# Chunk recurrence of a head pair: full 128x128 products with zero blocks, copies shared with ScalarE, state scaling on GpSimd

## The chip, the cores and the metric

The kernel runs on one core of a Trainium2 chip. The metric is the device time in microseconds (us) of one launch, as the median of several runs. TensorE does the matrix products (the profile calls it PE, and its weight loads PEld), VectorE is DVE, ScalarE is ACT, GpSimd is POOL, and SyncE (SP) issues the transfers.

## What is computed

One layer of a hybrid decoder trunk on 512 tokens of width 2048, all in float32: RMSNorm, one wide input projection, three groups of heads that work on parts of it, a SiLU gate on each, one output projection, and the residual. The change concerns the first group, twelve RWKV-7 heads of width 64. Cut to what matters:

```python
def reference(x, norm_g, w_in, ...):
    h = _rms(x, norm_g[l])
    proj = h @ w_in[l]                       # 2048 -> 7296 columns
    ...
    ya = _rwkv7(r, k, v, wd, ad, ...) * silu(ga)     # 12 heads of 64
    yb = _pool(pu, pool_w, pool_scale) * silu(pg)
    yc = _stick_breaking(qc, kc, vc, ...) * silu(gc) # 12 heads of 64
    return x + concatenate([ya, yb, yc]) @ w_out[l]

# in _rwkv7, for every token t and head:
sa    = state @ (-kk_t)
state = state * w_t + outer(sa, kk_t * a_t) + outer(v_t, k_t)
y_t   = state @ r_t
```

## The kernel before

**The foreground.** The projections are products of float32r numbers: every weight tile and the hidden state are split into a high and a low part, and three products per tile make the sum (`three`, line 396). The input projection is worked on tile by tile, 128 columns wide; a tile is 48 products of 512 columns into one PSUM bank (`pj`). Weights come by halves of a tile through SP's queue (`raw`); ScalarE casts the high part (`wh`) and VectorE subtracts for the low part (`wl`).

**The branches.** Between any two foreground products the program may insert a step of a branch. Each branch is a Python generator that yields the time at which its next step may join TensorE's queue (`need`, line 346); `pump` (line 359) runs those that are due. The clock for this is `Pace` (line 90), a rough account of every engine's work, kept while the program is written down. The order of the instructions thus comes from its costs, and a scheduler may move them further by priority; on the chip each engine works through its queue in that order.

**The recurrence.** Heads are taken in six pairs (`rwkv`, line 488); on the 128 partitions the first head of a pair has the low 64 (`lo`), the second the high 64 (`hi`). The 512 tokens are cut into 8 chunks of 64. Ahead of the recurrence, the products within a chunk (`gm`, line 571, four chunks to a bank) give the tiles `lt`, `rx` and part of `amr`; a triangular inverse is worked out in `lt`. The chunks then follow each other (line 669). Per chunk and head:

- `w`: `amr` by the state and values in `uv` (line 674); VectorE copies it to `wsb` (676).
- `se`: the state scaled by the chunk's decay, on VectorE (680).
- `y`, first half: the state by the r part of `amr` (684).
- `u`: `lt` by `wsb` (687); VectorE copies it into `uv` (689).
- `s`: `bkt` by `uv` (694); VectorE adds it to `se` and writes the next state into `uv` (696).
- `y`, second half: `uv` by `rx` (698); ScalarE copies it out to `yc` (699).

So w, u, s and the next w form a chain through TensorE and VectorE. Each product is 64 columns wide with 64 weights columns, one for each head; the two heads use different halves of the array. The PSUM tag `c` has three banks, shared by w, y, u and s.

Of the kernel before, what the change touches and what calls it, by code (L numbers as in the profile page):

```python
# [26 lines left out]
# columns of the packed per-channel vectors  # L27
# [14 lines left out]
# columns of the packed constants  # L42
# [8 lines left out]
# column tiles of the input projection, in the order in which they are worked on  # L51
NFIRST = 3
BANKS = {"pj": 2, "g": 3, "c": 3}
# [36 lines left out]
class Pace:  # L90
    """A rough clock of the engines, kept while the program is written down: it tells when a step of a
    branch can join TensorE's queue without TensorE having to wait for it."""
# [59 lines left out]
    def matmul(self, out, lhsT, rhs):  # L152
        n = self.free(rhs)
        m = self.free(lhsT)
        if rhs.dtype == F32R:
            c = max(n / 2400.0, m * 0.00083)
        else:
            c = max(4 * max(n, 64) / 2400.0, 0.1) * (0.6 if m <= 64 or rhs.shape[0] <= 64 else 1.0)
        self.now += c + 0.004
        self.ready[self.key(out)] = self.now + 0.28  # L160
# [20 lines left out]
class Timed:  # L181
    """An engine whose instructions the clock takes note of."""
# [21 lines left out]
def hybrid_trunk_kernel(ctx: ExitStack, tc: tile.TileContext, x, xT, w_in, w_out, vecs, consts, up_w, pool_w, out, tap=None):  # L204
# [64 lines left out]
    nvec = cp.tile([P, 14], F32, name="nvec")  # -w0, -a0, qn * 1/8  # L269
# [14 lines left out]
    # TensorE's clock rises while the first loads are under way  # L284
# [4 lines left out]
    # the input goes to places that the branches need only later  # L289
# [3 lines left out]
    for pl, tag, parts in ((ap, "q2", 1), (ap, "k2", 1), (ap, "w3", 1), (rp, "bk", 2), (rp, "bkt", 2), (rp, "rx", 2),  # L293
                           (rp, "uv", 2), (rp, "amr", 3), (ap, "wt", 2)):
        xt = pl.tile([P, parts, T], F32, tag=tag, name=name("x"))
# [192 lines left out]
    def rwkv(p):  # L488
# [54 lines left out]
        amr = rp.tile([P, NC_, 3, C], F32, tag="amr", name=name("amr"))  # L543
        for h, s in ((0, lo), (1, hi)):
# [7 lines left out]
        dve.tensor_tensor(amr[:, :, 2, :], r3, e[:, :, 1:], ALU.mult)  # L552
# [7 lines left out]
        lt = rp.tile([P, NC_, C], F32, tag="lt", name=name("lt"))  # L560
        ms = strict.rearrange("p (o t) -> p o t", o=1)
        mi = incl.rearrange("p (o t) -> p o t", o=1)
        for half in range(2):
            cs = slice(4 * half, 4 * half + 4)
            for h, s, other in quad:
                yield need(*([amr, bk] if half == 0 and h == 0 else []), tag="g")
                g = gb("gm")
                for j in range(4):
                    cc = 4 * half + j
                    rhs = amr[s, cc, 0:3:2, :] if h == 0 else amr[s, cc, 1:3, :]  # L570
                    mm(g[:, j * P:(j + 1) * P], bk[s, cc, :, :], rhs)
                g4 = g.rearrange("p (c a t) -> p c a t", c=4, a=2)
                dve.tensor_tensor(lt[s, cs, :], g4[s, :, 0, :], ms[s].to_broadcast([HD, 4, C]), ALU.mult)
# [6 lines left out]
        for h in range(2):  # L580
            for b in range(2):
                r0 = h * HD + b * B
                dma(out=s1v[:, :, h, b, :], in_=lt[r0:r0 + B, :, b * B:(b + 1) * B])
# [7 lines left out]
        # inverse of the 32 x 32 diagonal blocks, one block to a partition  # L591
        # (four copies of each block, every copy working on every fourth row)
# [21 lines left out]
        for h in range(2):  # L614
            for b in range(2):
                r0 = h * HD + b * B
                dma(out=lt[r0:r0 + B, :, b * B:(b + 1) * B], in_=s2v[:, :, h, b, :])

        # meanwhile: bonus, value token-major
# [20 lines left out]
        # merge to the 64 x 64 inverse: X12 = X1 N12 X2  # L640
        xt = tmp("xt")
        dve.transpose(xt, lt.rearrange("p c t -> p (c t)"))
        xt3 = xt.rearrange("p (c t) -> p c t", t=C)
# [3 lines left out]
        for cc in range(NC_):  # L647
            for h in range(2):
                r0 = h * HD
                mm(q1[r0 + B:r0 + 2 * B, cc * B:(cc + 1) * B], lt[r0:r0 + B, cc, B:C], xt3[r0:r0 + B, cc, 0:B])  # L650
# [5 lines left out]
        for cc in range(NC_):  # L656
            for h in range(2):
                r0 = h * HD
                mm(q2[r0:r0 + B, cc * B:(cc + 1) * B], w1[r0 + B:r0 + C, cc * B:(cc + 1) * B], lt[r0 + B:r0 + C, cc, B:C])
        for h in range(2):  # L660
            r0 = h * HD
            dve.tensor_copy(out=lt[r0:r0 + B, :, B:C], in_=q2[r0:r0 + B, :NC_ * B].rearrange("p (c t) -> p c t", t=B))

        # the state, chunk by chunk
# [4 lines left out]
        for cc in range(NC_):  # L669
            last = cc + 1 == NC_  # L670
            yield need(amr, uv, tag="c", margin=TIGHT)
            wps = cb("w")
            for h, s, o in quad:
                mm(wps[s, 0:C], amr[:, cc, h, :], uv[:, cc, h, :])
            wsb = rp.tile([P, C], F32, tag="wsb", bufs=2, name=name("wsb"))
            dve.tensor_copy(out=wsb, in_=wps[:, 0:C])
            if not last:
                se = rp.tile([P, C], F32, tag="se", bufs=2, name=name("se"))
                for h, s, o in quad:
                    dve.tensor_scalar(se[s, :], uv[s, cc, h, :], ec[s, cc:cc + 1], None, ALU.mult)  # L680
# [351 lines left out]
```

## Time and profile before

| | before |
|---|---|
| median of 3 runs | 1101.93 us (1100.72 to 1106.57) |
| span of the profiled execution, its own time | 1100.3 us |
| TensorE busy | 1074.3 us |
| VectorE busy | 751.3 us |
| ScalarE busy | 427.0 us |
| GpSimd busy | 168.7 us |
| mean granted TensorE clock | 0.982 |

The profile is of one execution. The span runs from its first instruction to its last; the page gives no longer time for that execution, and it lies 1.6 us under the median of the runs. A product of fp32 operands leaves two records in the trace, one of float32r leaves one, and a transpose leaves one. A record lasts from its start to the end of its results, so records overlap; how long TensorE is taken by something is read from the distance between starts.

### The profile page before, as it was taken

Reading aid. Unit: us, or ns where it says so; the run is one execution under the profiler, and the core shown is the slowest. Engines: PE = TensorE matmul, PEld = TensorE weight load, DVE = VectorE, ACT = ScalarE, POOL = GpSimd, SP = SyncE. Lnnn points to the kernel's source line nnn. Section 1 sums busy time; section 2 is a strip of 40 time slices with the busy share of each in tenths; the row PEclk is TensorE's granted clock in tenths of the full one; section 3 lists DMA queues with packets and bytes.
Section 4 is the critical chain, followed back from the end, with each engine's and each line's share of the span. In section 5 each row is a group of like instructions: output and inputs, shape, how many; then the busy total and the mean of one; then the engine's idle time right before and its main releaser. Section 6 shows DMA issues by size and latency. Waiting matters only on the chain.

```text
span 1100.3 us, 14737 instructions
## 1 busy us (share of the span) xinstructions
PE 1074.3 (98%) x5552; PEld 804.6 (73%) x5552; DVE 751.3 (68%) x1589; ACT 427.0 (39%) x670; POOL 168.7 (15%) x223
## 2 busy tenths in 40 slices
PE   9898989999999999999999999999999999999998
PEld 7676765677766877668775787667876677888886
DVE  5676876788877797877977788777986457233232
ACT  7362434244452453434543345423454235111111
POOL 2641122111121011210111102111012111000000
PEclk9899998999999999899998999999999999999999
DMA  8122321133211322113311133112331124444232
GB/s 316 38 82 82 101 73 40 57 82 101 77 54 42 104 82 87 39 59 106 86 63 58 60 103 87 63 39 68 115 92 58 39 85 161 161 153 134 96 136 75
DMA packets 57031, 97.70 MB, mean 89 GB/s; under 512 B 29184, under 2 KB 30592, under 8 KB 56960
## 3 DMA queue, kind: packets, MB, share of 16 engines
q1 hardware_dynamic: 56960, 96.76, 27.8%
q8 instruction: 44, 0.72, 0.3%
q14 instruction: 27, 0.22, 0.1%
HBM read 90.98 MB, written 5.77 MB: 88 GB/s over the span
## 4 chain that ended last, share of the span: by engine, by line
PE 73%; DVE 10%; issue 4%; POOL 2%; ACT 1%; DMA 1%; SPq 0%; POOLq 0%; DVEq 0%
PE pj L338 43%; PE oacc L338 15%; PE o L338 2%; DVE w L198 2%; PE z L338 2%; PE gm L338 2%; DVE wl L198 2%; PE y L338 2%; PE w L338 1%; POOL e L198 1%; PE u L338 1%; PE wT L342 1%; DVE xblk L198 1%; DVE pr L198 1%; PE s L338 1%
## 5 line engine op out<-in xcount | busy, mean ns | idle before, releaser
L338 PE MATMUL pj<-hh,wl 128*128 128x512 f32 x864 | 351.7, 407 | 1.0 <-DVE wl L198 1.0
L338 PE MATMUL pj<-hh,wh 128*128 128x512 f32 x864 | 350.0, 405 | 2.7 <-ACT wh L198 2.7
L338 PE MATMUL pj<-hl,wh 128*128 128x512 f32 x864 | 352.3, 408 | 0.0
L198 DVE TENSOR_TENSOR wl<-raw,wh 128x1024 fp32r<-128x1024 f32 x140 | 174.0, 1243 | 151.6 <-ACT wh L198 145.1
L198 ACT CAST wh<-raw 128x1024 fp32r<-128x1024 f32 x140 | 146.9, 1049 | 332.6 <-PE pj L338 204.2
L338 PEld LDWEIGHTS pj<-hh,wh 128*128 128x128 f32 x864 | 164.7, 191 | 39.3 <-issue 3.6
L338 PEld LDWEIGHTS pj<-hh,wl 128*128 128x128 f32 x864 | 164.4, 190 | 38.1 <-DVE wl L198 2.1
L338 PEld LDWEIGHTS pj<-hl,wh 128*128 128x128 f32 x864 | 164.3, 190 | 36.2 <-issue 1.4
L198 POOL TENSOR_SCALAR e<-e 128x512 f32<-128x512 f32 x28 | 49.3, 1760 | 365.0 <-ACT e L198 364.7
L338 PE MATMUL oacc<-wl,yh 128*128 128x512 f32 x256 | 100.2, 391 | 0.8 <-DVE wl L198 0.8
L338 PE MATMUL oacc<-wh,yh 128*128 128x512 f32 x256 | 99.7, 389 | 0.0
L338 PE MATMUL oacc<-wh,yl 128*128 128x512 f32 x256 | 99.7, 389 | 0.0
L198 POOL TENSOR_TENSOR d<-u 128x512 f32<-128x512 f32 x25 | 34.1, 1363 | 214.0 <-DVE u L198 178.9
L338 PEld LDWEIGHTS oacc<-wl,yh 128*128 128x128 f32 x256 | 48.1, 188 | 11.4 <-DVE wl L198 1.2
L338 PEld LDWEIGHTS oacc<-wh,yl 128*128 128x128 f32 x256 | 48.1, 188 | 10.2 <-issue 0.2
L338 PEld LDWEIGHTS oacc<-wh,yh 128*128 128x128 f32 x256 | 48.1, 188 | 9.8
L198 ACT ACTIVATE e<-e 128x512 f32<-128x512 f32 x50 | 31.5, 629 | 43.8 <-POOL e L198 43.4
L198 DVE TENSOR_TENSOR xblk<-xblk,pr 128x60 f32<-128x60 f32 (+8 forms) x180 | 42.0, 233 | 4.3
L198 DVE TENSOR_TENSOR_SCAN w<-kon,n 128x512 f32<-128x512 f32 (+3 forms) x48 | 39.4, 848 | 7.9 <-POOL n L198 7.6
L198 DVE TENSOR_TENSOR u<-pj,rstd 128x512 f32<-128x512 f32 x50 | 34.3, 686 | 13.9 <-PE pj L338 13.8
L198 DVE TENSOR_TENSOR pr<-xblk,nblk 128x60 f32<-128x60 f32 (+8 forms) x180 | 40.3, 224 | 4.5
L198 ACT ACTIVATE n<-n 128x512 f32<-128x512 f32 (+1 forms) x72 | 39.0, 557 | 1.3
(195 smaller groups left out, 1300.6 us busy)
## 6 DMA issues: line engine op xcount, KB each, us to landing
raw<-in_w_in SPq DMA_DIRECT2D x108, 512.0 KB
raw<-in_w_out SPq DMA_DIRECT2D x32, 512.0 KB
xr<-in_x SPq DMA_DIRECT2D x16, 256.0 KB
out<-xr SPq DMA_DIRECT2D x16, 256.0 KB
fr<-in_w_in SPq DMA_DIRECT2D x12, 256.0 KB
nblk<-s SPq DMA_DIRECT2D x24, 128.0 KB
x<-in_xT SPq DMA_DIRECT2D x5, 512.0 KB
x<-in_xT SPq DMA_DIRECT2D x3, 256.0 KB
```

The costliest lines, as they stand in the source:

```text
L198: return call(*args, **kw)
L338: pe.matmul(o, lhsT, rhs, start=start, stop=stop)
L342: pe.transpose(o, src, ident)
```

## The change

The tiles are laid out so that one product serves both heads of a pair. `amr` becomes 128 x 8 x 4 x 64, with zeros where a head's block would meet the other head's rows; `lt` gets a second block per head, zero outside the head's own rows. Both are allocated once for all pairs; the blocks that stay zero are filled once, and GpSimd clears the two others for every pair. In each chunk w, u, s and the two halves of y are one product each: 128 rows, 128 weight columns, and 128 columns streamed (64 for u). w, u and s of a chunk share one bank (`wus`, tag `c`, now two banks); y of four chunks shares the one bank of a new tag `y`, and is copied out once in four chunks. VectorE copies the first head's half of w and u, ScalarE the second's. `se` is computed on GpSimd, and so is the second head's r part of `amr`. gm uses all 128 rows. `Pace` charges 0.214 us for fp32 products with more than 64 weight columns.

```diff
-BANKS = {"pj": 2, "g": 3, "c": 3}
+BANKS = {"pj": 2, "g": 3, "c": 2, "y": 1}
...
-            c = max(4 * max(n, 64) / 2400.0, 0.1) * (0.6 if m <= 64 or rhs.shape[0] <= 64 else 1.0)
+            c = max(4 * max(n, 64) / 2400.0, 0.214 if m > 64 else 0.1) * (0.6 if m <= 64 or rhs.shape[0] <= 64 else 1.0)
...
+    amr_flat = rp.tile([P, NC_ * 4 * C], F32, tag="amr", name="amr")
+    amr = amr_flat.rearrange("p (c a t) -> p c a t", c=NC_, a=4)
+    lt = rp.tile([P, NC_, 2, C], F32, tag="lt", name="lt")
...
-        for h, s in ((0, lo), (1, hi)):
+        for h, s, other in quad:
+            pool.memset(amr[other, :, h, :], 0.0)
...
-        dve.tensor_tensor(amr[:, :, 2, :], r3, e[:, :, 1:], ALU.mult)
+        dve.tensor_tensor(amr[lo, :, 2, :], r3[lo], e[lo, :, 1:], ALU.mult)
+        pool.tensor_tensor(amr[hi, :, 3, :], r3[hi], e[hi, :, 1:], ALU.mult)
...
-                    rhs = amr[s, cc, 0:3:2, :] if h == 0 else amr[s, cc, 1:3, :]
-                    mm(g[:, j * P:(j + 1) * P], bk[s, cc, :, :], rhs)
+                    mm(g[:, j * P:(j + 1) * P], bk[:, cc, :, :], amr[:, cc, h:4:2, :])
...
-        xt = tmp("xt")
-        dve.transpose(xt, lt.rearrange("p c t -> p (c t)"))
+        xt = tmp("xt", NC_ * B)
+        xt3 = xt.rearrange("p (c t) -> p c t", t=B)
+        for h in range(2):
+            dve.transpose(xt3[h * HD:h * HD + B], lt[h * HD:h * HD + B, :, h, 0:B])
...
-            yield need(amr, uv, tag="c", margin=TIGHT)
-            wps = cb("w")
-            for h, s, o in quad:
-                mm(wps[s, 0:C], amr[:, cc, h, :], uv[:, cc, h, :])
+            yield need(amr_flat, uv, tag="c", margin=TIGHT)
+            wus = cb("wus")
+            wps, ups, sps = wus[:, 0:P], wus[:, P:P + C], wus[:, 2 * P:3 * P]
+            mm(wps, amr[:, cc, 0:2, :], uv[:, cc, :, :])
             wsb = rp.tile([P, C], F32, tag="wsb", bufs=2, name=name("wsb"))
-            dve.tensor_copy(out=wsb, in_=wps[:, 0:C])
+            dve.tensor_copy(out=wsb[lo, :], in_=wps[lo, 0:C])
+            act.copy(out=wsb[hi, :], in_=wps[hi, C:P])
             if not last:
                 se = rp.tile([P, C], F32, tag="se", bufs=2, name=name("se"))
                 for h, s, o in quad:
-                    dve.tensor_scalar(se[s, :], uv[s, cc, h, :], ec[s, cc:cc + 1], None, ALU.mult)
-            yield need(wsb, lt, tag="c", margin=TIGHT)
-            yps = cb("y")
-            for h, s, o in quad:
-                mm(yps[s, 0:C], uv[s, cc, h, :], amr[s, cc, 2, :], True, False)
-            ups = cb("u")
-            for h, s, o in quad:
-                mm(ups[s, 0:C], lt[s, cc, :], wsb[s, :])
-            for h, s, o in quad:
-                dve.tensor_copy(out=uv[s, cc, h, :], in_=ups[s, 0:C])
-            yield need(uv, tag=None if last else "c", margin=TIGHT + 0.1)
+                    pool.tensor_scalar(se[s, :], uv[s, cc, h, :], ec[s, cc:cc + 1], None, ALU.mult)
+            yield need(wsb, lt, tag="y" if cc % 4 == 0 else None, margin=TIGHT)
+            mm(ups, lt[:, cc, :, :], wsb)
+            if cc % 4 == 0:
+                ybank = bank("y", "y")
+            yps = ybank[:, (cc % 4) * P:(cc % 4 + 1) * P]
+            mm(yps, uv[:, cc, :, :], amr[:, cc, 2:4, :], True, False)
+            dve.tensor_copy(out=uv[lo, cc, 0, :], in_=ups[lo, :])
+            act.copy(out=uv[hi, cc, 1, :], in_=ups[hi, :])
+            yield need(uv, margin=TIGHT + 0.1)
             if not last:
-                sps = cb("s")
+                mm(sps, bkt[:, cc, :], uv[:, cc, :, :])
                 for h, s, o in quad:
-                    mm(sps[s, 0:C], bkt[:, cc, h * HD:(h + 1) * HD], uv[:, cc, h, :])
-                for h, s, o in quad:
-                    dve.scalar_tensor_tensor(uv[s, cc + 1, h, :], sps[s, 0:C], ec[s, cc:cc + 1], se[s, :], ALU.mult, ALU.add)
-            for h, s, o in quad:
-                mm(yps[s, 0:C], uv[:, cc, h, :], rx[:, cc, h, :], False, True)
-            act.copy(out=y[:, cc * C:(cc + 1) * C], in_=yps[:, 0:C])
+                    dve.scalar_tensor_tensor(uv[s, cc + 1, h, :], sps[s, h * C:(h + 1) * C], ec[s, cc:cc + 1], se[s, :], ALU.mult, ALU.add)
+            mm(yps, uv[:, cc, :, :], rx[:, cc, :, :], False, True)
+            if cc % 4 == 3:
+                y4 = ybank.rearrange("p (c h t) -> p c h t", c=4, h=2)
+                yo = y[:, (cc - 3) * C:(cc + 1) * C].rearrange("p (c t) -> p c t", t=C)
+                for h, s, o in quad:
+                    act.copy(out=yo[s], in_=y4[s, :, h, :])
...
+    for h, s, other in quad:
+        pool.memset(amr[other, :, 2 + h, :], 0.0)
+        pool.memset(lt[s, :, 1 - h, :], 0.0)
```

The change moves instructions, since `Pace` now has other costs and other steps. In the changed file the product helper is line 346 instead of 338. TensorE, a chunk in the second half of the second pair's recurrence, before (the names are tile<-operands, pj the projection products; x2 is one product for each head):

```order
L338 MATMUL s_2981<-uv_2505,bkt_1920 64x64 x2
L338 MATMUL y_2966<-rx_1921,uv_2505 64x64 x2
L338 MATMUL pj_2863<-hh_106,wh_2866 128x512
L338 MATMUL pj_2863<-hl_122,wh_2866 128x512
L338 MATMUL pj_2863<-hh_106,wl_2867 128x512
L338 MATMUL pj_2863<-hh_107,wh_2866 128x512
L338 MATMUL w_2993<-uv_2505,amr_1910 64x64 x2
L338 MATMUL y_3004<-amr_1910,uv_2505 64x64 x2
L338 MATMUL pj_2863<-hl_123,wh_2866 128x512
L338 MATMUL pj_2863<-hh_107,wl_2867 128x512
L338 MATMUL pj_2863<-hh_108,wh_2866 128x512
L338 MATMUL pj_2863<-hl_124,wh_2866 128x512
```

and now, a chunk of the same pair:

```order
L346 MATMUL wus_2851<-uv_2477,amr 128x128
L346 MATMUL y_2656<-amr,uv_2477 128x128
L346 MATMUL pj_2777<-hl_123,wh_2780 128x512
L346 MATMUL pj_2777<-hh_107,wl_2781 128x512
L346 MATMUL wus_2851<-wsb_2853,lt 128x64
L346 MATMUL pj_2777<-hh_108,wh_2780 128x512
L346 MATMUL pj_2777<-hl_124,wh_2780 128x512
L346 MATMUL pj_2777<-hh_108,wl_2781 128x512
L346 MATMUL wus_2851<-uv_2477,bkt_1894 128x128
L346 MATMUL y_2656<-rx_1895,uv_2477 128x128
L346 MATMUL pj_2777<-hh_109,wh_2780 128x512
L346 MATMUL pj_2777<-hl_125,wh_2780 128x512
```

Where four projection products stood between a w and its u, two stand here, and three between u and s; a w has its y directly behind it in both.

ScalarE in the changed kernel, the same stretch, with the semaphores that each instruction waits for (wh is the cast of the weights, yc the copy of y, e a step of a gate's sigmoid):

```order
L198 COPY wsb_2853<-wus_2851 64x64 [waits DVE_49]
L198 COPY uv_2477<-wus_2851 64x64 [waits DVE_49,Pool_49]
L198 COPY wsb_2879<-wus_2877 64x64 [waits DVE_49]
L198 COPY uv_2477<-wus_2877 64x64 [waits DVE_49,Pool_49]
L198 CAST wh_2930<-raw_2928 128x1024 [waits DMAHW3_49,PE_49]
L198 COPY yc_2592<-y_2656 64x256 [waits PE_49]
L198 COPY yc_2592<-y_2656 64x256
L198 COPY wsb_2907<-wus_2905 64x64 [waits DVE_49,Activation_49]
L198 ACTIVATE e_2921<-d_2918 128x512 [waits DVE_49]
L198 COPY uv_2477<-wus_2905 64x64 [waits DVE_49,Pool_49]
```

ScalarE's copies of wsb and uv wait for VectorE (DVE), whose copy of the other half comes first, and those of uv for GpSimd as well, which reads the old state for se. Before, ScalarE had one copy of y in each chunk here and none of wsb or uv.

## Rows read from the trace of the kernel before

**Rows 1.** The page, part 1: busy time of each engine.
```profile
PE 1074.3 (98%) x5552; PEld 804.6 (73%) x5552; DVE 751.3 (68%) x1589; ACT 427.0 (39%) x670; POOL 168.7 (15%) x223
```

**Rows 2.** Timeline of TensorE, a chunk (start us, duration us, engine, line, names, shapes).
```profile
338.91 0.39 PE L338 MATMUL pj<-hh,wl 128*128 128x512 f32 x1
339.23 0.34 PE L338 MATMUL s<-uv,bkt 128*64 128x64 f32 x4
339.40 0.29 PE L338 MATMUL y<-rx,uv 128*64 128x64 f32 x4
...
339.95 0.39 PE L338 MATMUL pj<-hl,wh 128*128 128x512 f32 x1
...
340.42 0.39 PE L338 MATMUL pj<-hh,wh 128*128 128x512 f32 x1
340.73 0.34 PE L338 MATMUL w<-uv,amr 128*64 128x64 f32 x4
...
341.60 0.39 PE L338 MATMUL pj<-hh,wl 128*128 128x512 f32 x1
...
342.06 0.40 PE L338 MATMUL pj<-hl,wh 128*128 128x512 f32 x1
342.39 0.33 PE L338 MATMUL u<-wsb,lt 64*64 64x64 f32 x4
...
342.98 0.39 PE L338 MATMUL pj<-hh,wh 128*128 128x512 f32 x1
```

**Rows 3.** Timeline of TensorE, a chunk whose heads' w stand apart.
```profile
211.29 0.40 PE L338 MATMUL pj<-hl,wh 128*128 128x512 f32 x1
211.62 0.33 PE L338 MATMUL w<-uv,amr 128*64 128x64 f32 x2
...
213.17 0.40 PE L338 MATMUL pj<-hl,wh 128*128 128x512 f32 x1
```

**Rows 4.** Timeline of TensorE, four products within a chunk (gm).
```profile
364.47 0.40 PE L338 MATMUL pj<-hl,wh 128*128 128x512 f32 x1
364.80 1.16 PE L338 MATMUL gm<-amr,bk 64*128 64x128 f32 x8
...
366.21 0.39 PE L338 MATMUL pj<-hh,wh 128*128 128x512 f32 x1
```

**Rows 5.** Timeline of TensorE: fp32 on the full array, transposes (vps) and pooling (po).
```profile
144.44 0.39 PE L338 MATMUL pj<-hh,wh 128*128 128x512 f32 x1
144.67 0.39 PE L338 MATMUL pj<-hl,wh 128*128 128x512 f32 x1
144.90 0.60 PE L342 MATMUL vps<-kon,u 128*128 128x128 f32 x4
...
145.57 0.40 PE L338 MATMUL pj<-hh,wh 128*128 128x512 f32 x1
...
920.10 0.40 PE L338 MATMUL oacc<-wh,yh 128*128 128x512 f32 x1
920.33 1.02 PE L338 MATMUL po<-pd,pw 128*128 128x512 f32 x2
...
921.42 0.40 PE L338 MATMUL oacc<-wh,yl 128*128 128x512 f32 x1
```

**Rows 6.** Groups by form: busy us, mean ns, idle before.
```profile
L198 DVE COPY wsb<-w 128x64 f32<-128x64 f32 x48 | 10.7, 223 | 20.2 <-PE w L338 19.5
L198 ACT COPY yc<-y 128x64 f32<-128x64 f32 x48 | 9.7, 203 | 64.2 <-PE y L338 64.0
L198 ACT CAST wh<-raw 128x1024 fp32r<-128x1024 f32 x140 | 146.9, 1049 | 332.6 <-PE pj L338 204.2 <-PE oacc L338 124.9 <-issue 3.3
L198 POOL TENSOR_SCALAR e<-e 128x512 f32<-128x512 f32 x28 | 49.3, 1760 | 365.0 <-ACT e L198 364.7
```

**Rows 7.** Timeline of TensorE at a wait, and windows: busy by engine, clock, DMA.
```profile
449.15 0.33 PE L338 MATMUL w<-uv,amr 128*64 128x64 f32 x2 [1.12 <-DVE uv L198]
...
440.00:460.00 20.00, 18.88 (x91) 12.61 (x91) 15.51 (x33) 10.85 (x20) 6.74 (x12) 0.83 0.08 27
```

More of the change, by code (lines that the diff above doesn't have):

```diff
@@ L293, in hybrid_trunk_kernel @@
     for pl, tag, parts in ((ap, "q2", 1), (ap, "k2", 1), (ap, "w3", 1), (rp, "bk", 2), (rp, "bkt", 2), (rp, "rx", 2),
-                           (rp, "uv", 2), (rp, "amr", 3), (ap, "wt", 2)):
-        xt = pl.tile([P, parts, T], F32, tag=tag, name=name("x"))
+                           (rp, "uv", 2), (None, "amr", 3), (ap, "wt", 2)):
+        if pl is None:
+            xt = amr_flat[:, 0:parts * T].rearrange("p (k t) -> p k t", k=parts)
+        else:
+            xt = pl.tile([P, parts, T], F32, tag=tag, name=name("x"))
         k = len(xk)
@@ L542, in rwkv @@
         bk = rp.tile([P, NC_, 2, C], F32, tag="bk", name=name("bk"))
-        amr = rp.tile([P, NC_, 3, C], F32, tag="amr", name=name("amr"))
-        for h, s in ((0, lo), (1, hi)):
+        for h, s, other in quad:
+            pool.memset(amr[other, :, h, :], 0.0)
             dve.scalar_tensor_tensor(bk[s, :, h, :], ba3[s], -1.0, ei3[s], ALU.mult, ALU.mult)
@@ L559, in rwkv @@
         rx = rp.tile([P, NC_, 2, C], F32, tag="rx", name=name("rx"))
-        lt = rp.tile([P, NC_, C], F32, tag="lt", name=name("lt"))
         ms = strict.rearrange("p (o t) -> p o t", o=1)
@@ L565, in rwkv @@
             for h, s, other in quad:
-                yield need(*([amr, bk] if half == 0 and h == 0 else []), tag="g")
+                yield need(*([amr_flat, bk] if half == 0 and h == 0 else []), tag="g")
                 g = gb("gm")
@@ L569, in rwkv @@
                     cc = 4 * half + j
-                    rhs = amr[s, cc, 0:3:2, :] if h == 0 else amr[s, cc, 1:3, :]
-                    mm(g[:, j * P:(j + 1) * P], bk[s, cc, :, :], rhs)
+                    mm(g[:, j * P:(j + 1) * P], bk[:, cc, :, :], amr[:, cc, h:4:2, :])
                 g4 = g.rearrange("p (c a t) -> p c a t", c=4, a=2)
-                dve.tensor_tensor(lt[s, cs, :], g4[s, :, 0, :], ms[s].to_broadcast([HD, 4, C]), ALU.mult)
+                dve.tensor_tensor(lt[s, cs, h, :], g4[s, :, 0, :], ms[s].to_broadcast([HD, 4, C]), ALU.mult)
                 dve.tensor_tensor(amr[other, cs, h, :], g4[other, :, 0, :], ms[other].to_broadcast([HD, 4, C]), ALU.mult)
@@ L582, in rwkv @@
                 r0 = h * HD + b * B
-                dma(out=s1v[:, :, h, b, :], in_=lt[r0:r0 + B, :, b * B:(b + 1) * B])
+                dma(out=s1v[:, :, h, b, :], in_=lt[r0:r0 + B, :, h, b * B:(b + 1) * B])
         for half in range(2):
@@ L616, in rwkv @@
                 r0 = h * HD + b * B
-                dma(out=lt[r0:r0 + B, :, b * B:(b + 1) * B], in_=s2v[:, :, h, b, :])
+                dma(out=lt[r0:r0 + B, :, h, b * B:(b + 1) * B], in_=s2v[:, :, h, b, :])
         while ("v", p) not in got:
@@ L638, in rwkv @@
         yield soon(lt)
-        xt = tmp("xt")
-        dve.transpose(xt, lt.rearrange("p c t -> p (c t)"))
-        xt3 = xt.rearrange("p (c t) -> p c t", t=C)
+        xt = tmp("xt", NC_ * B)
+        xt3 = xt.rearrange("p (c t) -> p c t", t=B)
+        for h in range(2):
+            dve.transpose(xt3[h * HD:h * HD + B], lt[h * HD:h * HD + B, :, h, 0:B])
         yield need(xt, tag="g")
@@ L649, in rwkv @@
                 r0 = h * HD
-                mm(q1[r0 + B:r0 + 2 * B, cc * B:(cc + 1) * B], lt[r0:r0 + B, cc, B:C], xt3[r0:r0 + B, cc, 0:B])
+                mm(q1[r0 + B:r0 + 2 * B, cc * B:(cc + 1) * B], lt[r0:r0 + B, cc, h, B:C], xt3[r0:r0 + B, cc, :])
         for h in range(2):
@@ L658, in rwkv @@
                 r0 = h * HD
-                mm(q2[r0:r0 + B, cc * B:(cc + 1) * B], w1[r0 + B:r0 + C, cc * B:(cc + 1) * B], lt[r0 + B:r0 + C, cc, B:C])
+                mm(q2[r0:r0 + B, cc * B:(cc + 1) * B], w1[r0 + B:r0 + C, cc * B:(cc + 1) * B], lt[r0 + B:r0 + C, cc, h, B:C])
         for h in range(2):
             r0 = h * HD
-            dve.tensor_copy(out=lt[r0:r0 + B, :, B:C], in_=q2[r0:r0 + B, :NC_ * B].rearrange("p (c t) -> p c t", t=B))
+            dve.tensor_copy(out=lt[r0:r0 + B, :, h, B:C], in_=q2[r0:r0 + B, :NC_ * B].rearrange("p (c t) -> p c t", t=B))
         done[("mid", p)] = True
@@ L882, in finish @@
             got[(kind, i)] = u
-    first = [cb("first") for _ in range(NFIRST)]
+    first = [bank(("c", "c", "y")[n], "first") for n in range(NFIRST)]
     for kq in range(KT // KQ):
@@ L931, in split_y @@
         dve.tensor_tensor(yl[k], yt[k], yh[k].bitcast(F32), ALU.subtract)
-    tags = ("c",) * 3 + ("g",) * 3 + ("pj",) * 2
+    tags = ("c", "c", "y") + ("g",) * 3 + ("pj",) * 2
     used = 0
```

## The prediction

> **What bounds the kernel now.** I read the page first: engine shares, slices, costliest groups. TensorE is busy for 98% of the span, VectorE for 68%, ScalarE for 39%, GpSimd for 15% [rows 1]. No other engine is near, so the question about every edit is what it does to TensorE's queue, and the other engines matter only where TensorE has to wait for them. A busy TensorE is not an efficient one, so I then read TensorE's timeline around the chunk recurrence. Its records are pipelined, and the honest price of a group of small products is the distance between the starts of the projection products around it: from the last one before the group to the second one after it, less two plain steps. A plain step from projection product to projection product is 0.23 us (144.44 to 144.67 in [rows 5]). By that rule, from [rows 2], where the rows left out are projection products and, behind w, its y:
>
> - s with its y: 338.91 to 339.95 is 1.04, less 0.46: 0.58 us.
> - w with its y: 340.42 to 341.60 is 1.18, less 0.46: 0.72 us.
> - u: 342.06 to 342.98 is 0.92, less 0.46: 0.46 us.
>
> A chunk in which w and y stand together thus costs 1.76 us of TensorE. The other kind stands in [rows 3]: the two heads' w are apart (two records each), so they no longer run side by side. From 211.29 to 213.17 is 1.88 us with three projection products in it, so w and y cost 1.88 - 0.69 = 1.19, and the chunk 1.19 + 0.46 + 0.58 = 2.23 us. Much of each price is not streaming: the group starts 0.31 to 0.33 after the projection product before it instead of 0.23, and four records of s are through in 0.17 (339.23 to 339.40) where s and y together cost 0.58.
>
> **The change, part by part.**
>
> *The chunk products.* Before, a chunk has 10 products of 64 rows or columns (8 in a last chunk), 468 in all; now 5 (4), 48 x 5 - 6 = 234, all on the full array. Old cost: between 1.76 and 2.23 us per chunk; I take 1.95, because both kinds and chunks in between (w apart from y) are common: 48 x 1.95 = 94 us, with the ends 84 and 107. New cost: no full fp32 product of 128 columns stands in the trace, so I bound it. The nearest rows are the fp32 transposes [rows 5]: four of them on the full array cost 144.67 to 145.57 = 0.90 - 0.46 = 0.44 us, 0.11 for each record; and po, a true fp32 product of 512 columns on the full array, is two records and costs 920.10 to 921.42 = 1.32 - 0.46 = 0.86, that is 0.215 for each 128 columns. Both say that a full product of 128 columns, two records, costs 0.22, and that a group on the full array pays nothing at its ends. The other end is gm [rows 4], fp32 with 64 rows: four products cost 364.47 to 366.21 = 1.74 - 0.46 = 1.28, 0.32 each; at that price the saving would be 94 - 75 = 19 us. I take 0.22, since both the rows on the full array have it. For u, which streams only 64 columns, 0.11 to 0.22 is open (half the columns, the same weights); I take 0.22, and the low end would give 5 us more. New cost 234 x 0.22 = 52 us. Term: **-42 us**, ends -19 and -60.
>
> Against this speaks what the same rows show of side-by-side work: the four records of s, both heads, take from 339.23 to 339.40, 0.17 us, less than the 0.22 of one full product. If only this counted, 234 full products would cost 234 x 0.05 = 12 us more than the pairs they replace. The Trainium skill ("TensorE: Matmul & The Clock Gate", Part 3, "The mechanism") says this as a rule: small products in different row and column groups of the array run at once, so filling the array with zero blocks gives away what tiling had won. By the rule alone the sum would go up by those 12 us; by the distances between projection products in rows 2 and 3, which hold the ends of each group as well, it goes down by 42. I go by the distances.
>
> *The products within a chunk (gm).* They too become full. 24 groups of four; one that stands alone costs 1.28 before [rows 4] and 4 x 0.22 = 0.88 now; where groups touch, little changes. Between 0 and 24 x 0.4 = 10 us; I take **-5 us**.
>
> *The copies.* wsb and uv were VectorE's alone. Now VectorE copies the low half and ScalarE the high half, but the order shows that ScalarE's copy waits for VectorE's, so they are in series: VectorE 0.22 and then ScalarE about 0.20 [rows 6]. From w to u TensorE must now allow: second record 0.11 after the first, 0.27 to its end (the four transposes of [rows 5] last 0.60, of which 3 x 0.11 are starts), 0.22 and 0.20 for the copies, 0.80 us together, and three handovers between engines, for which I assume 0.05 each: 0.95 us. The tight chunk in the order excerpt leaves w, y and two projection products, 0.22 + 0.22 + 0.46 = 0.90; between u and s stand u and three, 0.91, against the same 0.95. So a tight chunk waits about 0.1 us, and about a third of the chunks in the new order are so tight: 2 us. On ScalarE the copies stand behind casts of weights (1.05 us each [rows 6]), which wait for TensorE themselves; where one is directly ahead of a copy, or ahead of the yc copies that release the single y bank, TensorE waits up to about 1 us. I allow half a microsecond per pair for that: 3 us. VectorE is rid of one uv copy and both se per chunk, which gains nothing directly, since TensorE's work covers VectorE; ScalarE takes on two copies for each y copy of before (0.20 each, 20 us in all, less what fewer y copies save), hidden while it is 39% busy. Term: **+5 us**, ends 0 and +30 (two waits of 0.3 in every chunk).
>
> *se on GpSimd.* 84 small multiplications, and uv may not be overwritten until both are done. They have the time from one uv to the next, about 1 us, and start at once if GpSimd is free. It is not when a clamp of e (1.76 us [rows 6]) is ahead; then VectorE's uv copy waits, and everything behind it on VectorE. Bound: no cost to 12 such meetings of 1 us; taken as 0, because GpSimd has only 15% of work and the order places most se right behind each other. The zero fills and GpSimd's half of r lie beside projection products; if they came last before gm, at most a clamp's 1.76 us per pair, 11 us in all. SP's queue issues the same transfers in both kernels.
>
> *Stalls and clock.* At 449.15 w waits 1.12 us for uv, which stands behind attention's work on VectorE, and the stretch around it has a granted clock of 0.83 [rows 7], so part of it ran at 1.2 GHz instead of 2.4. Five of the 20 us windows from 160 us on read 0.83 or 0.91 (at 160, 320, 440, 580 and 700); the missing shares make 0.69 x 20 = 14 us. The order there is near the same: 0, with -14 (all gone) and +5 as ends.
>
> Sum: 1100.3 - 42 - 5 + 5 = 1058 us on the span of the profiled execution. The median of the runs is 1.6 us above that span, so the forecast is **1060 us**.
>
> **The rivals.**
> *Waits take the place of the saved work.* Both copies and se now cross three engines, each with an in-order queue. It decides if TensorE waits on average 1 us more per chunk (47 us over 48). For it: the copies are in series, a cast of 1.05 is often close ahead, and TensorE's slack between steps is smaller in the new order. If every chunk met one cast (1.05) and half a clamp of e (0.9), that is 1.9 x 48 = 91, less 47: 1146; the mild form, 1.1 us per chunk, 1106. Against: the pacing code moves a step back until its inputs should be ready, and only a third of the chunks are tight. Half of that price, 0.5 us per chunk, leaves a gain: 1080.
> *Tiling was worth more than its ends.* If the gaps around the groups come from the change between number formats, not from the tile's shape, they stay and the 12 us are added: 1100.3 + 12 + 1.6 = 1114. Against it: the full fp32 groups in [rows 5] show no such ends. It is where the rule of the Trainium skill's page "TensorE: Matmul & The Clock Gate" leads.
> *More than forecast.* u at half price (-5), all gm at 1.28 (-5), the stalls and their slow clock gone (-10): 1040.
> *That the change doesn't do what it says* is excluded: the new order has the 234 products on the full array.
>
> **How the numbers follow.** Forecast (1045 to 1072): 0.60. Better, about 1040: 0.12. Partly eaten by waits, about 1080: 0.15. Waits take it all, 1106 and above: 0.08. Tiling's price, 1114: 0.05. The range takes in the first three up to 1085 and leaves out the slower ones and the far end below 1040. A measurement tells about 0.5% from no change (1096 to 1107 here). Faster 0.85, same 0.06 (the mild edge of the waits), slower 0.09.
>
> **What would show it.** Right: chunk products with half the records, groups that start 0.23 after the projection product before them, a w, y, u, s, y set near 1.1 us of TensorE, VectorE some 34 us less busy. Wrong: idle time of TensorE in front of u or s put down to ScalarE, or in front of w to VectorE, of over 0.3 us per chunk; full products that cost 0.3 us or more; more stretches with a clock below 1.

## The result and the profile after

The changed kernel takes 1108.05 us (median of 10 runs, 1104.90 to 1114.35) against 1101.33 for the kernel before beside it (10 runs): a ratio of 1.0062, with a 95% interval of 1.0039 to 1.0085. It is slower by 0.6%, where 1060 had been forecast. Its profiled execution took 1104.90 us, the least of the ten; its span is 1102.7 us against 1100.3, so the accounts below are those of a run 3 us under the median. From its page come part 1, the slices of the granted clock (tenths of full speed) and the shares of the chain that ended last:

```profile
PE 1046.6 (95%) x5084; PEld 818.1 (74%) x5084; DVE 717.1 (65%) x1463; ACT 446.4 (40%) x742; POOL 241.1 (22%) x329
PEclk9998998999999999799999999999999999999999
PE 59%; DVE 18%; issue 5%; POOL 5%; DMA 3%; ACT 3%; POOLq 0%; SPq 0%; DVEq 0%; ACTq 0%
```

Against [rows 1], TensorE is busy 27.7 us less, VectorE 34.2 less (the forecast had 34), GpSimd 72 more. But TensorE is idle for 1102.7 - 1046.6 = 56.1 us, where it was 26.0. The mean granted clock is 0.978 against 0.982 (the views of the cores). Taking (1 - clock) x span as an estimate of the time given to the half clock, 24.3 us against 19.8, what is left of the busy time is TensorE's work at full clock:

| us | span | idle | half clock | work |
|---|---|---|---|---|
| before | 1100.3 | 26.0 | 19.8 | 1054.5 |
| after | 1102.7 | 56.1 | 24.3 | 1022.3 |
| difference | +2.4 | +30.1 | +4.5 | -32.2 |

So TensorE's work did fall, and idle time has taken the place of what was saved. What it waited for, TensorE's list of waits tells (us in total, times, longest), first after, then the largest of before:

```profile
PE q L346 <- DVE xt L198: 12.1, 3, 5.9
PE wT L350 <- ACT w L198: 8.6, 8, 2.0
PE wus L346 <- ACT wsb L198: 6.9, 5, 2.4
PE pj L346 <- ACT wh L198: 5.0, 1, 5.0
PE wus L346 <- DVE uv L198: 2.9, 6, 0.9
PE wus L346 <- ACT uv L198: 2.9, 5, 1.0
```

```profile
PE w L338 <- DVE uv L198: 4.9, 5, 1.1
PE q L338 <- DVE xt L198: 3.5, 1, 3.5
```

With the smaller rows of both lists, the waits in front of chunk products (w, u, s, y) went from 5.8 to 14.9 us, those of the merge (q) from 4.0 to 14.0, of the attention's transposes (wT) from 0.5 to 8.6, of the projections (pj) from 3.7 to 6.4: +30 in all. Only a third is in the chunks.

**The products cost what was forecast where nothing waits.** TensorE's timeline of s with its y, then a w alone:

```profile
487.99 0.39 PE L346 MATMUL pj<-hh,wl 128*128 128x512 f32 x1
488.22 0.38 PE L346 MATMUL wus<-uv,bkt 128*128 128x128 f32 x2
...
488.90 0.40 PE L346 MATMUL pj<-hl,wh 128*128 128x512 f32 x1
...
604.06 0.40 PE L346 MATMUL pj<-hh,wl 128*128 128x512 f32 x1
604.30 0.39 PE L346 MATMUL wus<-uv,amr 128*128 128x128 f32 x2
...
604.75 0.40 PE L346 MATMUL pj<-hl,wh 128*128 128x512 f32 x1
```

By the rule of the distances s and y cost 0.91 - 0.46 = 0.45 us (0.58 in [rows 2]) and w 0.69 - 0.46 = 0.23: 0.22 to 0.23 each, and each group starts 0.23 to 0.24 behind the projection product. The Trainium skill ("TensorE: Matmul & The Clock Gate", Part 3, "The mechanism") states that small products in different tiles of the array overlap, and the 0.17 us for the four records of s in [rows 2] agree. That zero blocks would therefore cost time is what the prediction drew from it, and this does not show here: TensorE's work fell.

**But the handover often leaves a short wait that is not counted as idle.** The same group in another chunk:

```profile
343.47 0.40 PE L346 MATMUL pj<-hl,wh 128*128 128x512 f32 x1
343.53 0.21 ACT L198 COPY uv<-wus 64x64 f32<-64x64 f32 x1 [0.90 <-DVE uv L198]
343.79 0.30 PEld L346 LDWEIGHTS wus<-uv,bkt 128*128 128x128 f32 x2 [0.35 <-ACT uv L198]
343.79 0.49 PE L346 MATMUL wus<-uv,bkt 128*128 128x128 f32 x2
...
344.57 0.39 PE L346 MATMUL pj<-hh,wh 128*128 128x512 f32 x1
```

343.47 to 344.57 is 1.10 - 0.46 = 0.64 us: 0.19 more than above, since the weights (uv) come from ScalarE's copy, which waited for VectorE's. TensorE reads as busy throughout, because the projection product's modelled end covers the gap. TensorE's weight loads waited for ScalarE's wsb and uv 27 and 26 times, so about half of the chunks met this. Such waits are not new: with those for VectorE, the weight loads of chunk products waited 46 times and 21.8 us before, 66 times and 32.7 us now.

For s with y the dear case is the common one. Of the groups of s and y that stand alone between projection products, the median cost is 0.63 us (34 groups) where it was 0.59 (32); w alone went from 0.47 (9) to 0.26 (25), u alone from 0.47 (35) to 0.35 (25). Over all groups that hold chunk products only (680 of 936 records before, 368 of 468 now), scaled to all records, the chunk products cost an estimated 104 us before and 83 now, or 70 without the waits that the profile lists as idle. The forecast had 94 and 52.

**Where three queues stand behind one another** it is dear. All engines, around the largest wait for wsb:

```profile
619.71 1.16 POOL L198 TENSOR_SCALAR se<-uv,ec 64x64 f32<-64x64 f32 x1
620.67 0.22 DVE L198 COPY wsb<-wus 64x64 f32<-64x64 f32 x1
620.96 1.49 POOL L198 TENSOR_SCALAR e<-e 128x512 f32<-128x512 f32 x1
622.49 1.29 ACT L198 ACTIVATE e<-e 128x512 f32<-128x512 f32 x2 [2.93 <-POOL e L198]
623.80 0.21 ACT L198 COPY wsb<-wus 64x64 f32<-64x64 f32 x1
624.06 0.43 PE L346 MATMUL wus<-wsb,lt 128*128 128x64 f32 x2 [2.44 <-ACT wsb L198]
```

VectorE's half of wsb was there at 620.89. ScalarE's half, 0.21 us of work, stood behind two e activations; the first waited for GpSimd's clamp of e, which stood behind se. TensorE was idle for 2.44 us.

**The merge** is the other kind: an order that asks too early.

```profile
432.66 0.17 DVE L198 TENSOR_TENSOR xblk<-xblk,pr 128x8 f32<-128x8 f32 x1
...
433.12 0.55 SPq L212 DMA_DIRECT2D s<-xblk  x1
...
435.99 0.39 PE L346 MATMUL pj<-hh,wh 128*128 128x512 f32 x1
439.80 0.43 DVE L198 STREAM_TRANSPOSE xt<-lt 32x256 f32<-32x256 f32 x1 [5.33 <-DMA lt<-s]
440.29 0.31 PE L346 MATMUL q<-xt,lt 32*32 32x32 f32 x2 [3.91 <-DVE xt L198]
...
442.30 0.63 PE L346 MATMUL pj<-hh,wl 128*128 128x512 f32 x1
442.72 0.63 PE L346 MATMUL pj<-hh,wh 128*128 128x512 f32 x1
```

The inverse ends on VectorE at 432.83 and its two transfers (out to s, back to lt) are through when xt starts, 7.0 us later. TensorE's queue has only 14 projection products, 3 us, in between. So it idles for 3.91 us, and then runs at half clock: the projection step is 0.42 (442.30 to 442.72) instead of 0.23, and the stretch reads 0.76, where the window of [rows 7] read 0.83:

```profile
440.00:460.00 20.00, 17.49 (x116) 11.02 (x116) 8.76 (x20) 6.07 (x12) 5.04 (x7) 0.76 0.11 36
```

In the kernel before, the same pair has 61 projection products between the end of the inverse and q, and q waits for nothing:

```profile
407.18 0.17 DVE L198 TENSOR_TENSOR xblk<-xblk,pr 128x8 f32<-128x8 f32 x1
...
423.62 0.57 PE L338 MATMUL q<-xt,lt 32*32 32x32 f32 x24
```

Counted so in all six pairs, the kernel before has 23, 53, 61, 61, 60 and 60 projection products there, the change 8, 31, 14, 40, 45 and 43. q waits over 2 us for xt in the pairs with 23 before, and with 8, 31 and 14 now.

### The profile page after: what moved, and what is told of

Read it like the earlier page. It is cut to its first block, busy times and chain, and to the rows that moved or that the text cites. A ratio compares the mean times of both kernels' runs of the same rounds, so it can differ in the third digit from the quotient of the medians.

```text
span 1102.7 us, 13967 instructions
## 1 busy us (share of the span) xinstructions
PE 1046.6 (95%) x5084; PEld 818.1 (74%) x5084; DVE 717.1 (65%) x1463; ACT 446.4 (40%) x742; POOL 241.1 (22%) x329
## 4 chain that ended last, share of the span: by engine, by line
PE 59%; DVE 18%; issue 5%; POOL 5%; DMA 3%; ACT 3%; POOLq 0%; SPq 0%; DVEq 0%; ACTq 0%
PE pj L346 30%; PE oacc L346 15%; DVE wl L198 4%; DVE w L198 3%; PE wus L346 3%; PE o L346 2%; PE gm L346 2%; POOL e L198 2%; DVE xblk L198 2%; DVE pr L198 2%; DMA s<-xblk 2%; PE y L346 2%; PE z L346 1%; DVE n L198 1%; POOL d L198 1%
## 5 line engine op out<-in xcount | busy, mean ns | idle before, releaser
L198 DVE TENSOR_TENSOR wl<-raw,wh 128x1024 fp32r<-128x1024 f32 x140 | 176.3, 1260 | 163.9 <-ACT wh L198 158.0
L198 POOL TENSOR_SCALAR se<-uv,ec 64x64 f32<-64x64 f32 x84 | 49.6, 590 | 88.5 <-DVE uv L198 84.2
L198 DVE TENSOR_TENSOR pr<-xblk,nblk 128x60 f32<-128x60 f32 (+8 forms) x180 | 44.0, 244 | 3.8 <-DMA xblk<-s 0.4
L198 DVE SCALAR_TENSOR_TENSOR uv<-wus,ec,se 64x64 f32<-64x64 f32 x84 | 23.7, 282 | 28.9 <-PE wus L346 27.3
```

What stands on the lines that cost most here:

```text
L198: return call(*args, **kw)
```

## The experiments

All edits are to the changed kernel unless the kernel before is named. Ratios are to the kernel before, with their 95% intervals.

### Copies and scaling back on VectorE (e1, e2, e3)

The planner is told what it was told in the change, so that TensorE's order hardly moves: four fifths of the records of the branches stand behind as many projection products as in the change, the others at most 13 off. e1 has the two copies, e2 the scaling, e3 both.

```diff
-            act.copy(out=wsb[hi, :], in_=wps[hi, C:P])
+            pace.record("act", "copy", wsb[hi, :], [wps[hi, C:P]])
+            nc.vector.tensor_copy(out=wsb[hi, :], in_=wps[hi, C:P])
...
-                    pool.tensor_scalar(se[s, :], uv[s, cc, h, :], ec[s, cc:cc + 1], None, ALU.mult)
+                    pace.record("pool", "tensor_scalar", se[s, :], [uv[s, cc, h, :], ec[s, cc:cc + 1]])
+                    nc.vector.tensor_scalar(se[s, :], uv[s, cc, h, :], ec[s, cc:cc + 1], None, ALU.mult)
```

> Both halves of wsb and uv copied by VectorE, as the kernel before did; the planner's books still say ScalarE, so that TensorE's order stays nearly that of the change. Theory A (the saved TensorE work comes back as waits at the copies that cross to ScalarE): TensorE's waits for ScalarE's wsb and uv (6.9 + 2.9 us) and for the y bank (1.3) go, with part of the half clock behind them; 1092 to 1098 us against 1108. Theory B (the copies matter little; the planner's clock, now nearer the truth for the chunk products, puts the merge and other steps too early): within 4 us of 1108, the merge's 12.1 us of waiting for xt still there. Theory C (any move of the order shifts the time by some us, either way): anything from 1098 to 1118 with the waits at other places.

> The two se of a chunk back on VectorE, again with the planner's books as in the change. Theory A: GpSimd's 49.6 us of se (0.59 each) stand ahead of the clamps of e, and ScalarE waits for those with a wsb copy queued behind it (2.4 us at 624); without them 3 to 8 us faster than 1108. Theory B: within 4 us of 1108. A rival within A: VectorE is the bound of the recurrence, and two more instructions of about 0.15 us on it per chunk make it slower, 1108 to 1114.

> Full products with the copies and the scaling all on VectorE, the planner's books as in the change: what the products alone are worth. Theory A: the sum of the two single moves, 1085 to 1095, faster than the kernel before by 0.5 to 1.5 %. Theory B: 1100 to 1108, since the merge's and the transposes' waits (12.1 and 8.6 us) stay. If the full products themselves were no gain, TensorE's busy time would stay at the 1046.6 us of the change and the time near 1108 with few waits.

Measured: e1 1100.97 us, 0.9987 (0.9972 to 1.0002); e2 1099.31, 0.9965 (0.9945 to 0.9985); e3 1099.85, 0.9973 (0.9958 to 0.9989). By the medians each is 7 to 9 us faster than the change (8 to 11 by the ratios to the kernel before), and both together no more than one. The chain at 624, which needs both links, would explain that; it is not shown, since the order moved a little too. All three times miss the ranges of theories A and B, e2 and e3 by less than a microsecond. In e2 the copies are still ScalarE's, but no wait for wsb is longer than 0.7 us (2.4 in the change). TensorE's waits in e2:

```profile
PE q L346 <- DVE xt L198: 10.6, 3, 5.9
PE wT L350 <- ACT w L198: 7.7, 7, 2.0
...
PE wus L346 <- ACT uv L198: 2.9, 5, 0.8
PE wus L346 <- ACT wsb L198: 2.8, 6, 0.7
```

The larger part stays: with everything on VectorE (e3) q still waits 12.0 for xt and wT 11.2 for w, TensorE is idle 51.4 us, and the full products alone are worth 0.3%, not 4%. The waits left are those of theory B. Theory A explains about 8 of the 48 us by which the forecast was missed. (On VectorE one se of e2 takes 0.32 us in the mean, not the 0.15 that was expected.)

### The merge later (e4)

```diff
-        yield soon(lt)
+        yield need(lt, margin=4.0)
```

> The change as it is, only the planner's margin in front of the merge raised from -1.5 to 4.0 us behind the landing it expects for lt, so that the transposes of lt and q stand later in the queues. Theory B: TensorE's 12.1 us of waiting for xt and VectorE's 21.3 us for lt go, and with them the half clock behind the stalls at 166 and 440 (6.8 and 10.2 us long, half of it lost): 1090 to 1098 us. Theory A: the copies' waits remain; the q wait was hidden slack and something else ends later instead, 1104 to 1110. It can also be slower, if the later merge delays the chunk recurrence of its pair and the recurrence of the next pair with it: above 1112.

Measured: 1119.56 us, 1.0146 (1.0118 to 1.0173), and q still waits 12.3 us for xt, 4 times. The edit did not do what it was for: in the first three pairs q stands behind the same number of projection products as before the edit (388, 778, 1180, counted in the trace), while much else in the order moved. It says nothing on theory B, but was the first sign of how much a moved order can cost.

### The planner's price (e5, e6, e7)

The change also edits a line of the planner: 0.214 us for each full product, about what it takes. Before, a narrow product was charged 0.064, although a pair took 0.46.

```diff
-            c = max(4 * max(n, 64) / 2400.0, 0.214 if m > 64 else 0.1) * (0.6 if m <= 64 or rhs.shape[0] <= 64 else 1.0)
+            c = max(4 * max(n, 64) / 2400.0, 0.214 if m > 64 else 0.1) * (0.6 if n <= 128 or m <= 64 or rhs.shape[0] <= 64 else 1.0)
```

That is e5; e6 has, besides, the two copies and the scaling as `dve.tensor_copy` and `dve.tensor_scalar`, in the planner's books too. e7 edits the kernel before:

```diff
-            c = max(4 * max(n, 64) / 2400.0, 0.1) * (0.6 if m <= 64 or rhs.shape[0] <= 64 else 1.0)
+            c = max(4 * max(n, 64) / 2400.0, 0.1) * (2.0 if n == 64 else 0.6 if m <= 64 or rhs.shape[0] <= 64 else 1.0)
```

> The change as it is, only the planner's price of a product of up to 128 columns put back to 0.128 us (2 x 0.064, what two of the narrow products had been charged), although it takes 0.22 on TensorE. Theory B2 (the low price was a hidden slack: the planner's clock fell behind TensorE by about 1 us in each chunk, so whatever it placed by time, the merge and the attention's transposes too, came late enough; the true price took that slack away): TensorE's waits at q (12.1 us) and wT (8.6) shrink to 6 or less together, and the time falls to 1075 to 1090 us. Theory A (the crossings to ScalarE and GpSimd): the waits at wus stay at about 13 us, the time within 5 us of 1108. Theory C (order's luck): any place from 1098 to 1118, the waits moved about but not gone.

> Full products with the copies and the scaling on VectorE, and the planner's price of a product of up to 128 columns at 0.128 us. Theory B2: both losses gone, so the 32 us of TensorE's work that the change saves by its trace show: 1068 to 1080 us. Theory C: 1090 to 1105, like the run with the products alone (1099.9).

> The kernel before, only the planner's price of a 64-column product raised from 0.064 to 0.213 us, which is nearer to what TensorE takes (0.46 for a pair). The products, engines and copies are those of before. Theory B2: the waits of the change appear here too, at q and wT: 1112 to 1125 us, 1 to 2 % slower than before. Theory A: no difference beyond the order's luck, 1097 to 1107.

Measured: e5 1084.61 us, 0.9858 (0.9821 to 0.9895); e6 1079.90, 0.9813 (0.9767 to 0.9858); e7 1156.03, 1.0502 (1.0465 to 1.0539). No instruction of an engine differs between e5 and the change, only the order: 23 us. Of e5's waits, q's shrank from 12.1 us to 3.4, wT's stayed (8.6 and 8.3):

```profile
PE wT L350 <- ACT w L198: 8.3, 9, 1.9
...
PE q L346 <- DVE xt L198: 3.4, 3, 2.2
```

In e7 the old narrow products lose 56 us, with a wait at q like that of the change, little at wT (2.8 us), and a half clock that costs 49.6 us where it was 19.8 (its TensorE's largest waits, part 1 and clock slices):

```profile
PE q L338 <- DVE xt L198: 13.9, 5, 3.7
PE pj L338 <- DVE u L198: 6.3, 3, 3.1
...
PE 1104.6 (96%) x5552; PEld 822.7 (71%) x5552; DVE 747.5 (65%) x1589; ACT 425.8 (37%) x670; POOL 169.1 (15%) x223
PEclk9899989999999999999889996999959999999999
```

All three moved the way of theory B2, and the times of e5 and e6 lie in its ranges, that of e6 at the edge. But the waits at wT did not shrink in e5, and e7 lies 31 us above its range. The control beside them speaks against the theory.

### Luck of the order (e8, e9, e14, e15)

```diff
-MARGIN = 1.5
+MARGIN = 1.4    # 1.6 in e14 and e15
```

> A control for the order's luck: the kernel before with the planner's general margin at 1.4 instead of 1.5 us, an edit that means nothing for the engines but gives another order. Theory C, luck of some us: off by more than 6 us to either side. Theories A and B2 need this to be small: within 4 us of before.

> The change with the planner's general margin at 1.4 instead of 1.5 us, the edit that alone made the kernel before 1.4 % faster: how far luck of the order carries at the true price. Theory B2 (the true price is the loss): 1095 to 1120, so not below the 1084.6 that the low price gave. Theory C (luck alone): as likely at 1085 as at 1108.

> The change at its true price with the general margin at 1.6: the third order. Theory B2: 1095 to 1135, above every order of the price 0.128 (1079.9 to 1084.9). Theory C: below 1090 is as likely as not.

> The kernel before with the general margin at 1.6: the third order at the low price. Theory B2: 1080 to 1105, with the half clock of 3 to 18 us making the difference. Theory C: up to 1130.

Measured: the kernel before at 1.4 (e8) 1085.52 us, 0.9863 (0.9827 to 0.9899), and at 1.6 (e15) 1138.58, 1.0332 (1.0291 to 1.0374); the change at 1.4 (e9) 1132.93, 1.0271 (1.0213 to 1.0329), and at 1.6 (e14) 1092.14, 0.9921 (0.9892 to 0.9950). An edit of 0.1 us in a margin moves either kernel by 15 to 36 us. Theory B2's ranges were missed in all four, and e15 missed theory C's too. The order's luck is thus as large as the 23 us between e5 and the change; only e7 moved by more. In e8 no slice of the clock reads below 9 tenths; its half clock costs (1 - 0.997) x 1082.0 = 3.2 us instead of 19.8:

```profile
PE 1060.4 (98%) x5552; PEld 798.2 (74%) x5552; DVE 752.2 (70%) x1589; ACT 427.7 (40%) x670; POOL 185.4 (17%) x223
PEclk9999999999999999999999999999999999999999
```

In e15 q waits for xt in all six pairs, with 24 to 28 projection products behind the inverse; in e8 in none, with 43 to 63. The order repeats itself with each pair, so one bad meeting comes six times. In e9 it is the transposes. The row of e15, then that of e9:

```profile
PE q L338 <- DVE xt L198: 15.5, 6, 2.8
```

```profile
PE wT L350 <- ACT w L198: 22.6, 12, 3.3
```

### Price by margin (e10, e11, e12, e13, e16, e17, e18)

The two edits crossed: price 0.128 and margin 1.4 (e10) or 1.6 (e17); the same with all on VectorE (e12, e18). And three single steps: in e11 the low price is 0.085, in e13 (e6 otherwise) the margin within a chunk is 0.30, and in e16, the kernel before, the price is in between. The diff has the changed lines of e11 (set against e5), e13 and e16, those of a price cut to its factor.

```diff
-(0.6 if n <= 128 or m <= 64 or rhs.shape[0] <= 64 else 1.0)
+(0.4 if n <= 128 else 0.6 if m <= 64 or rhs.shape[0] <= 64 else 1.0)
...
-TIGHT = 0.05
+TIGHT = 0.3
...
-(0.6 if m <= 64 or rhs.shape[0] <= 64 else 1.0)
+(1.0 if n == 64 else 0.6 if m <= 64 or rhs.shape[0] <= 64 else 1.0)
```

> The change with both edits: a product of up to 128 columns at 0.128 us in the planner's books, and the general margin at 1.4. Theory B2: again under 1095, so that the two orders with the low price lie below the two with the true one. Theory C: anywhere from 1080 to 1110.

> The change with a product of up to 128 columns at 0.085 us in the planner's books, still lower than the 0.128 that gave 1084.6. Theory B2: slack again a little larger, waits at q and wT no more than the 12.4 us of that run, 1070 to 1088; where slack is too large the recurrence of a pair ends later and holds up the next, which would show as waits at the end of the program. Theory C: anywhere from 1080 to 1110.

> Full products with copies and scaling on VectorE, price 0.128, general margin 1.4: the second order for the fastest kernel so far (1079.9). Theory B2 and TensorE's 32 us of saved work: 1065 to 1085. Theory C: 1080 to 1105.

> Full products with copies and scaling on VectorE, price 0.128, and the margin within a chunk at 0.30 instead of 0.05 us. If the 13.2 us of waits in front of the chunk products are tight margins: under 5 us of them, 1068 to 1076. If slack costs more than it saves, as at the price 0.085: 1085 to 1105 with the waits elsewhere.

> The kernel before with a 64-column product at 0.107 us in the planner's books, between the 0.064 of before and the 0.213 that gave 1156. Theory B2 (the loss grows with the price): 1100 to 1140. Theory C: no trend, 1085 to 1156 alike; below 1095 would speak against B2.

> The change, price 0.128, general margin 1.6. If the price is a cause: 1078 to 1090, below the 1092 that the true price gives at this margin. If the low price's orders were luck: anywhere from 1080 to 1135, above 1095 as likely as not.

> Full products with copies and scaling on VectorE, price 0.128, general margin 1.6. If the price is a cause: 1075 to 1090. If luck: anywhere from 1080 to 1135. If the crossings of the change cost something by themselves: 0 to 9 us below the run beside it.

Measured: e11 1105.78 us, 1.0028 (1.0005 to 1.0051): theory B2 missed, so a still lower price is not better. e13 1087.76, 0.9878 (0.9839 to 0.9917): with more slack the chunk products still wait 15.9 us (12.1 in e6, not 13.2), which speaks against a tight margin as the cause of these waits. e16 1105.10, 1.0029 (1.0006 to 1.0052): no growth beyond 0.3% from 0.064 to 0.107. The grid, as ratios to the kernel before, with 95% intervals of 0.2 to 0.6% to either side:

| products, price | margin 1.4 | 1.5 | 1.6 | mean |
|---|---|---|---|---|
| before, 0.064 | 0.986 (e8) | 1 | 1.033 (e15) | 1.007 |
| the change, 0.214 | 1.027 (e9) | 1.006 | 0.992 (e14) | 1.008 |
| the change, 0.128 | 0.984 (e10) | 0.986 (e5) | 1.000 (e17) | 0.990 |
| all on VectorE, 0.128 | 0.984 (e12) | 0.981 (e6) | 0.988 (e18) | 0.985 |

The low price is better at two margins and worse at the third (e17: 1102.90 against 1092.14, above the 1090 expected if the price is a cause; e18 lies 1.5 us above the same bound). That it helps is not shown. VectorE is ahead of the crossings by 0 to 11 us at each margin (1084.85 to 1084.48, 1084.61 to 1079.90, 1102.90 to 1091.47); its price is in the planner's books here, so the order moved as well, and such a difference is within the order's luck. And over three orders each, the change and the kernel before are level in the mean, with a spread of 3.5% and more among the orders of each.

The same accounts as above (idle = span - busy; half clock = (1 - clock) x span; work = the rest) for one run of each:

| us | idle | half clock | work |
|---|---|---|---|
| narrow: e8, before, e15 | 21.6, 26.0, 38.5 | 3.2, 19.8, 31.9 | 1057, 1055, 1070 |
| change, 0.214: e9, after, e14 | 72.9, 56.1, 48.0 | 27.2, 24.3, 9.8 | 1032, 1022, 1030 |
| change, 0.128: e10, e5, e17 | 44.0, 46.8, 53.7 | 10.8, 14.1, 25.3 | 1024, 1024, 1023 |
| VectorE, 0.128: e12, e6, e18 | 44.9, 38.6, 48.2 | 5.4, 10.8, 10.9 | 1031, 1029, 1031 |

This is what holds in every order of the table: at the same margin, full products take 25 to 48 us off TensorE's work and raise its idle time by 9 to 51 us. Over all twenty traces of this case the work is 1054 to 1070 us with narrow products and 1022 to 1032 with full ones. What swings is the idle time, by 17 us among the narrow orders and 25 among those of the change, and the half clock, from 3 to 32 us.

## Why the prediction was wrong, step by step

- *Chunk products, -42, and gm, -5.* Right in sign, too large: TensorE's work fell by 32, not 47. The new price was right where nothing waits (0.22 forecast, 0.22 to 0.23 measured), but most groups of s and y carry a short wait inside them, as at 343.47. By the estimate over all groups, the narrow products cost 104 us, not 94, and the full ones 70, not 52, without the waits listed as idle: 0.30 us each, which the prediction had named as a sign of being wrong. (The low end of -19 is set against the middle of the old cost; against its low end, 84, it would be -9.)
- *Copies, +5 (0 to +30).* In the range, too small: the waits in front of chunk products rose by 9 us, and moving copies or se back goes with 7 to 9 us of time. The prediction looked for a cast ahead of ScalarE's copy. The dearest meeting was another: se, GpSimd's clamp, ScalarE's e, then the copy.
- *se on GpSimd, 0.* The bound of 12 us held, the 0 did not, as far as one order shows: e2 is 8.7 us faster (1108.05 - 1099.31), the same microseconds as those of the copies, since both moves together gain no more than one. The step looked for se behind a clamp and for VectorE's copy behind se; at 624 it was the clamp that stood behind se, and ScalarE's queue behind the clamp.
- *Stalls and clock, 0 (-14 to +5).* **This is the step that failed.** It read: "The order there is near the same". It was not: from before to after, the projection products between the inverse and q went from 61 to 14 in the third pair and fell in every other, and the price line alone gives another order (e5 against the change, 23 us, or 2% of the time). After, q, wT and the projections wait 21 us more than before, and the half clock takes 4.5 more. The forecast of the span was -42 us, the measured difference +2.4: of the 44 us between them, 25 are idle time beyond the 5 that the copies' term had, 15 are work that was not saved, and 4.5 are half clock. The range for that step should have been near that of e8 and e15, -15 to +36 us for an edit that changes nothing but the order, which is about as large as the saving itself. Yet it is not this order's luck alone: idle time rose at every margin.
- *The rivals.* "Waits take the place of the saved work" was right in kind. Its mild form, 1106, came close to 1108 by luck (it is a span, without the 1.6 us that the forecast adds): it had 1.1 us in each chunk, 53 in all, where the chunk products' listed waits rose by 9 and the rest lay elsewhere. "Tiling was worth more than its ends" gave 1114, near in number and wrong in kind.
- *The range.* It is given as 1045 to 1072 and, with the milder rivals, up to 1085; the time lies outside both.

Which part of the 7 us between the two kernels as given is the change's and which is the order's cannot be told from one order of each. What can be told: its work on TensorE is less in every order tried, and in the mean of three orders the kernel is no faster. Why the full products leave more idle time, after the crossings are taken away (e12, e6, e18 against e8, before, e15: 10 to 23 us more), stays open: the trace shows waits at the chunk products, the merge and the transposes, and neither the margin in the chunk (e13) nor the price removed them in every order.

The fastest kernel is e6, full products with all copies on VectorE at the price 0.128: 1079.90 us, 0.9813 (0.9767 to 0.9858). It is the best of many orders and ahead of the kernel before, but by 6 us only of the best of the three orders tried of that (e8).

## What to carry to other kernels

Where a planner sets the order, a price in it is part of the change: test a few orders of each kernel (a margin moved a little) before a difference of 1 or 2% is put down to the instructions. Work taken off a full engine shows in the time only if what feeds it can come sooner; list the steps whose inputs arrive from another queue or by a transfer, and ask what stands between. And a small copy moved to an engine with time to spare stands behind whatever its queue waits for, as the 0.21 us of wsb did for 2.44 us at 624.

## What was not expected of the hardware

One se, 64 x 64, takes 590 ns on GpSimd in the mean, and 248 on VectorE in the kernel before. The rows of after and of before (groups by form):

```profile
L198 POOL TENSOR_SCALAR se<-uv,ec 64x64 f32<-64x64 f32 x84 | 49.6, 590 | 88.5 <-DVE uv L198 84.2
```

```profile
L198 DVE TENSOR_SCALAR se<-uv,ec 64x64 f32<-64x64 f32 x84 | 20.8, 248 | 2.1
```

And a wait can cost more than its length: the 3.91 us at 440 were followed by steps at half clock. Length alone does not tell: in the kernel before the 1.12 us at 449 [rows 7] were followed by half clock too, while after the waits of 2.28 us at 307 and of 2.44 us at 624 the granted clock stayed full. Between two orders of one kernel the half clock alone differs by 29 us (e8 and e15, 3.2 and 31.9).
